# Stick-breaking attention: the sums of key blocks 2 and 3 formed on VectorE for three of five score tiles, two weight units' low parts and q's high part issued later

## The chip, the cores and the metric

The kernel runs on one core of one Trainium2 chip. The metric is the device time of one execution in microseconds (us). The engines named here are TensorE (PE; its weight loads are shown apart as PEld), VectorE (DVE), ScalarE (ACT), GpSimd (POOL) and SyncE (SP, which issues the DMAs).

## What is computed

A decoder of two layers on 512 tokens of width 1024: a Mamba-2 layer, then a layer of stick-breaking attention, each with a gated convolutional feed-forward and an embedding gate. The change lies in the attention alone, 16 heads of 64:

```
for blk in range(seq // SB_BLOCK):                    # 4 blocks of 128 queries
    z = einsum("bthd,bshd->bhts", q[:, q0:q1], k[:, :q1]) * scale
    causal = (q0 + arange(SB_BLOCK))[:, None] > arange(q1)[None, :]
    log_beta = log_sigmoid(z)
    log_keep = where(causal, log_sigmoid(-z), 0.0)
    log_rest = cumsum(log_keep, axis=3, reverse=True) - log_keep
    w = where(causal, exp(log_beta + log_rest), 0.0)
    outs.append(einsum("bhts,bshd->bthd", w, v[:, :q1]))
```

Each weight takes the sum of `log_keep` over all later keys. That sum runs over the rest of the key's own block of 128 and over all of the later blocks.

## The kernel before

*Precision.* Every float32 operand of a matmul is split into a high part, rounded to the type that TensorE reads (`fp32r`), and a low part, the remainder. A product is three matmuls: high by low, low by high, high by high (L241 to L243). Weights come by DMA in units of eight 128x128 blocks (`raw`). For the attention GpSimd multiplies them by a gain (L108), ScalarE makes the high part `whi` (L126), VectorE the low part `wlo` (L133). Three buffers exist for each of `raw`, `whi` and `wlo`, so a unit's DMA starts when the low part of the unit three before it is done.

*The stage.* `pair(p, ...)` runs eight times, once for two heads. Keys lie on the partitions and queries on the columns. There are five score tiles `zs` of 128x512: tile 0 holds key block 2 of both heads (256 columns each), tiles 1 and 2 hold blocks 3 and 1 of one head each (128 and 384 columns), tiles 3 and 4 hold block 0 of one head each (512 columns). A pair goes so:

1. `scores` (L792): score matmuls of all tiles on TensorE, with the mask.
2. ScalarE forms `e`, VectorE adds `max(z, 0)` to it (`sums`, L910). That is the negative of `log_keep`, up to the mask.
3. `parts` (L915) splits `e`: VectorE casts to `sh`, GpSimd subtracts for `sl`.
4. `att_b` (L830): TensorE adds to each score tile the sum over later keys. For the tile's own block that is a matmul of `ntri` (a triangle of -1) with `sh` and `sl`, for each later block one of `nones` (all -1). The table `more` lists these: columns of the score tile from, to, the operand pair and its first column. `s2`, `sa`, `sc` are the parts of tiles 0, 1, 2. Then ScalarE takes the exponential, which gives the weights `w`, and makes their high parts. VectorE makes the low parts afterwards.
5. `att_c` (L863): TensorE multiplies weights and values, for the pair before, within the next pair.

Between these TensorE runs the projections of the next pair: its k product behind the first `att_c`, its q product ahead of `att_b`, its v product behind `att_b`. So in pairs 1 to 6 TensorE's order is scores, `att_c` (head 0), k, `att_c` (head 1), q (with the transposes of the values in it), `att_b`, v. Pair 0 has no `att_c` yet; pair 7 has no projections left and runs parts of the output product instead.

*What sets the order.* Within the eight pairs the order on TensorE, VectorE, ScalarE and GpSimd is that of the program text (a manual schedule for four engines). Each engine takes its queue strictly in that order. What this change moves is therefore visible in `pair`: `parts(3)`, `parts(4)`, then q's evacuation from PSUM (`qk_evac`, L755, into `t`) and its high part on ScalarE, then `att_b`, then a list of low parts on VectorE (`wt.low`, `low`), and at the end the values' evacuation (`v_evac`, L770). `order` gives the sequence of the tiles in `att_b`: 1, 0, 2, 3, 4 in pairs 1 to 6, and 2, 1, 0, 3, 4 in pairs 0 and 7. `new` are the three weight units fetched in a pair: the next pair's values, then k and q of the pair after.

Of the kernel before, what the change touches and what calls it, by code (L numbers as in the profile page):

```python
# [15 lines left out]
P = 128  # L16
# [130 lines left out]
def tile_yoco(ctx: ExitStack, tc: tile.TileContext, xT, pT, prm, cst, csb, wdt, wts, out, dbg=None):  # L147
# [605 lines left out]
    def qk_evac(acc, scale):  # L753
        t = S("t", 2)
        V.scalar_tensor_tensor(out=t, in0=acc, scalar=scale, in1=n_kv.r, op0=ALU.mult, op1=ALU.mult)  # L755
        return t

    def high(src):
        hi = H(F32R, name="hi")
        A.copy(out=hi, in_=src)  # L760
        return src, hi

    def low(src, hi, lo=None):
        lo = lo or H(F32R, name="lo")
        V.tensor_tensor(out=lo, in0=src, in1=hi.bitcast(F32), op=ALU.subtract)  # L765
        return hi, lo

    def v_evac(p, acc):
        vs[p] = S("t", 2, name="v")
        V.tensor_tensor(out=vs[p], in0=acc, in1=n_kv.r, op=ALU.mult)  # L770
# [56 lines left out]
    def like(n, t):  # L827
        return t.rearrange("p (a b) -> p a b", a=2) if n == 0 else t

    def att_b(zs, sp, order):  # L830

        s2, sa, sc = sp[0], sp[1], sp[2]
        more = {
            1: [(384, 512, sa, 0), (256, 512, s2, 0)],
            0: [(128, 256, sa, 0), (384, 512, sc, 0)],
            2: [(384, 512, sc, 0), (256, 512, s2, 256)],
            3: [(128, 512, sa, 128), (256, 512, s2, 0), (384, 512, sa, 0)],
            4: [(128, 512, sc, 128), (256, 512, s2, 256), (384, 512, sc, 0)],
        }
        ws = {}  # L840
        for n in order:
            z = zs[n]
            if n:
                mm = [(z, ntri, s_) for s_ in sp[n]]
                for c0, c1, t_, f0 in more[n]:
                    mm += [(z[:, c0:c1], nones, s_[:, f0:f0 + c1 - c0]) for s_ in t_]
            else:
                mm = [(z[:, i], ntri, s_[:, i * 256:(i + 1) * 256]) for s_ in sp[n] for i in range(2)]
                for c0, c1, t_, f0 in more[n]:
                    i, c = divmod(c0, 256)  # L850
                    mm += [(z[:, i, c:c + c1 - c0], nones, s_[:, f0:f0 + c1 - c0]) for s_ in t_]
            for k, (o_, l_, r_) in enumerate(mm):
                PE.matmul(o_, lhsT=l_, rhs=r_, start=False, stop=k == len(mm) - 1, skip_group_check=True)  # L853
            w = S("d", 6, name="w") if n < 3 else S("c", 3, name="w")
            A.activation(out=like(n, w), in_=z, func=AF.Exp)
            ws[n] = high(w)
        return ws

    o_t = []
# [37 lines left out]
    def pair(p, ws, accs):  # L897
# [7 lines left out]
        def exps(n):  # L905
            es[n] = S("d", 6, name="e") if n < 3 else S("c", 3, name="e")
            A.activation(out=like(n, es[n]), in_=zs[n], func=AF.Abs)  # L907
            A.activation(out=es[n], in_=es[n], func=AF.Exp, scale=-1.0)  # L908
# [6 lines left out]
        def parts(n):  # L915
            sp[n] = H(F32R, name="sh"), H(F32R, name="sl")
            V.tensor_copy(out=sp[n][0], in_=es[n])  # L917
            G.tensor_tensor(out=sp[n][1], in0=es[n], in1=sp[n][0].bitcast(F32), op=ALU.subtract)  # L918

        exps(2)  # L920
        exps(0)
        if p == 7:
# [48 lines left out]
        parts(4)  # L971
        if p < 7:
            wt.high(new[1])
            qt = high(qk_evac(acc, 0.125))
        order = (1, 0, 2, 3, 4) if 0 < p < 7 else (2, 1, 0, 3, 4)
        ws = att_b(zs, sp, order)
        wt.low(new[0])
        ws[order[0]] = low(*ws[order[0]])
        if 0 < p < 7:
            ks[p + 1] = low(*kt)  # L980
        ws[order[1]] = low(*ws[order[1]])
        if p < 7:
            qs[p + 1] = low(*qt)
        ws[order[2]] = low(*ws[order[2]])
        if p:
            o_t.append(low(*oh, lo=S("ot", 8, F32R)))
        ws[3] = low(*ws[3])
        if p < 7:
            wt.low(new[1])
            wt.high(new[2])  # L990
        ws[4] = low(*ws[4])
        if p < 7:
            wt.low(new[2])
            v_evac(p + 1, proj("v", p + 1))
        return ws

    qa, ka = aux_bank("qa"), aux_bank("ka")
# [151 lines left out]
```

## Time and profile before

| | |
|---|---|
| Median of 3 runs | 1525.64 us (1523.31 to 1528.34) |
| The profiled execution | 1525.47 us, its span 1523.6 us |
| TensorE busy | 1490.8 us, 98% of the span |
| VectorE busy | 983.3 us, 65% |
| ScalarE busy | 771.1 us, 51% |
| GpSimd busy | 315.5 us, 21% |
| Mean granted clock of TensorE | 0.995 of full speed |

The eight pairs of the attention lie between 830.8 and 1049 us of the span. The shares are means over stages with different limits, so the attention is read by itself: how full TensorE is there, what it waits for, and at what time the other engines finish what it waits for. Ends of matmuls are modelled; the starts are what the rows are read by.

### The profile page before, as it was taken

The page shows a single profiled execution, that of the slowest core. Times are in us where ns is not written, and L with a number is a line of the kernel's source. Part 1 is how long each engine was busy: PE and PEld are TensorE (multiplying, and loading weights), DVE is VectorE, ACT ScalarE, POOL GpSimd, SP SyncE. Part 2 cuts the span into 40 slices and gives each one's busy share as a digit, 9 for nine tenths or more (in the row PEclk, how much of TensorE's full clock was granted, in tenths as well). Part 3 has the DMA queues.
Part 4 walks back from the last instruction along what each step waited for, and adds up shares of the span by engine and source line. Part 5 has one row for each costly group of instructions (what it writes and reads, how often), then busy time and mean ns, then how long its engine had stood idle before and what let it go on. Part 6 is the DMA issues. An engine that isn't in the chain of part 4 may idle for free.

```text
span 1523.6 us, 18513 instructions
## 1 busy us (share of the span) xinstructions
PE 1490.8 (98%) x7140; PEld 1226.6 (81%) x7140; DVE 983.3 (65%) x1338; ACT 771.1 (51%) x1186; POOL 315.5 (21%) x225
## 2 busy tenths in 40 slices
PE   8999999999999999999999999998999999999997
PEld 5878777788888888888888888887888888888886
DVE  6987888864577777732366676775677677742344
ACT  5466565643344444422356788886444444432243
POOL 0022332532111111100113444521311111100111
PEclk9999999999999999999999999999999999999999
DMA  5334333333333333333332112122233333333321
GB/s 186 95 126 132 103 104 118 104 97 97 91 98 91 104 92 102 102 105 97 97 89 83 42 56 69 42 66 72 89 100 96 98 96 98 97 104 97 97 83 55
DMA packets 43624, 143.69 MB, mean 94 GB/s; under 512 B 4848, under 2 KB 5104, under 8 KB 43536
## 3 DMA queue, kind: packets, MB, share of 16 engines
q1 hardware_dynamic: 43536, 142.51, 30.8%
q8 instruction: 56, 0.92, 0.3%
q14 instruction: 32, 0.26, 0.1%
HBM read 140.32 MB, written 2.16 MB: 94 GB/s over the span
## 4 chain that ended last, share of the span: by engine, by line
PE 73%; ACT 8%; DVE 8%; POOL 5%; issue 5%; DMA 1%; SPq 0%; POOLq 0%; DVEq 0%; ACTq 0%
PE acc L241 22%; PE acc L242 22%; PE acc L243 22%; PE z L853 1%; DVE wlo L133 1%; POOL y L543 1%; DVE c L347 1%; ACT e L908 1%; ACT d L515 1%; DVE e L911 1%; ACT e L907 1%; POOL d L519 1%; ACT whi L126 1%; POOL xrd L479 1%; PE z L821 1%
## 5 line engine op out<-in xcount | busy, mean ns | idle before, releaser
L242 PE MATMUL acc<-lo,whi 128*128 128x512 f32 x1808 | 704.9, 390 | 0.0
L241 PE MATMUL acc<-hi,wlo 128*128 128x512 f32 x1776 | 703.9, 396 | 0.0
L243 PE MATMUL acc<-hi,whi 128*128 128x512 f32 x1776 | 693.3, 390 | 0.0
L133 DVE TENSOR_TENSOR wlo<-raw,whi 128x1024 fp32r<-128x1024 f32 (+1 forms) x241 | 308.5, 1280 | 190.2 <-ACT whi L126 186.5
L242 PEld LDWEIGHTS acc<-lo,whi 128*128 128x128 f32 x1808 | 340.3, 188 | 70.8 <-issue 2.9
L243 PEld LDWEIGHTS acc<-hi,whi 128*128 128x128 f32 x1776 | 334.2, 188 | 70.8
L241 PEld LDWEIGHTS acc<-hi,wlo 128*128 128x128 f32 x1776 | 334.3, 188 | 70.4 <-issue 3.2
L126 ACT CAST whi<-raw 128x1024 fp32r<-128x1024 f32 (+1 forms) x241 | 251.9, 1046 | 270.5 <-PE acc L243 212.4
L347 DVE SCALAR_TENSOR_TENSOR c<-t,pm,c 128x511 f32<-128x511 f32 (+2 forms) x248 | 186.7, 755 | 5.1 <-ACT c L342 1.2
L260 POOL TENSOR_TENSOR acc_sq<-acc_sq,sq 128x512 f32<-128x512 f32 x53 | 76.9, 1451 | 406.1 <-ACT sq L257 357.7
L665 POOL TENSOR_TENSOR hf<-th,c 128x512 f32<-128x512 f32 x44 | 57.4, 1305 | 422.1 <-DVE c L347 411.0
L342 ACT ACTIVATE c<-t,pm 128x512 f32<-128x512 f32 x112 | 91.2, 815 | 26.0 <-DVE t L340 25.7
L222 ACT CAST hi<-hf 128x512 fp32r<-128x512 f32 x44 | 27.1, 620 | 123.2 <-POOL hf L665 123.2
L340 DVE TENSOR_TENSOR t<-acc,r 128x512 f32<-128x512 f32 x112 | 76.5, 684 | 17.8 <-PE acc L243 14.3
L223 DVE TENSOR_TENSOR lo<-hf,hi 128x512 fp32r<-128x512 f32 x44 | 30.4, 690 | 72.1 <-ACT hi L222 72.1
L918 POOL TENSOR_TENSOR sl<-e,sh 128x512 fp32r<-128x512 f32 x40 | 59.6, 1499 | 71.7 <-DVE sh L917 70.6
L662 ACT ACTIVATE th<-c 128x512 f32<-128x512 f32 x44 | 27.8, 632 | 78.3 <-DVE c L347 78.3
L108 POOL TENSOR_TENSOR raw<-raw,pm 128x1024 f32<-128x1024 f32 x20 | 39.2, 1960 | 56.4 <-DMA raw<-in_wts 48.1
L663 DVE SCALAR_TENSOR_TENSOR th<-th,c 128x512 f32<-128x512 f32 x44 | 30.4, 692 | 30.6 <-ACT th L662 30.6
L911 DVE SCALAR_TENSOR_TENSOR e<-z,e 128x512 f32<-128x512 f32 x40 | 26.7, 685 | 32.8 <-ACT e L939 32.6
L515 ACT ACTIVATE d<-d,tok 128x128 f32<-128x128 f32 x128 | 43.5, 390 | 7.2 <-DMA d<-rows 7.1
L765 DVE TENSOR_TENSOR lo<-w,hi 128x512 fp32r<-128x512 f32 x40 | 37.2, 938 | 11.8 <-ACT hi L760 11.8
(205 smaller groups left out, 1481.4 us busy)
## 6 DMA issues: line engine op xcount, KB each, us to landing
raw<-in_wts SPq DMA_DIRECT2D x239, 512.0 KB, 3.6
d<-rows SPq DMA_DIRECT2D x32, 256.0 KB, 4.3
x_k<-in_xT SPq DMA_DIRECT2D x16, 256.0 KB, 5.4
out<-yo SPq DMA_DIRECT2D x3, 512.0 KB, 3.3
p_k<-in_pT SPq DMA_DIRECT2D x4, 256.0 KB, 2.8
raw<-in_wts SPq DMA_DIRECT2D x2, 256.0 KB, 4.4
out<-yo SPq DMA_DIRECT2D x2, 256.0 KB, 4.0
pm<-in_prm SPq DMA_DIRECT2D x1, 312.0 KB, 6.4
```

Source lines behind the costliest of these rows:

```text
L126: self.nc.scalar.copy(out=self.units[u][0][:, part], in_=raw[:, part])
L133: self.nc.vector.tensor_tensor(out=lo[:, part], in0=raw[:, part], in1=hi[:, part].bitcast(F32), op=ALU.subtract)
L241: PE.matmul(acc, lhsT=wl, rhs=xh, start=start and n == 0, stop=False)
L242: PE.matmul(acc, lhsT=wh, rhs=xl, start=False, stop=False)
L243: PE.matmul(acc, lhsT=wh, rhs=xh, start=False, stop=stop and n == len(ks) - 1)
L260: self.eng.tensor_tensor(out=self.acc, in0=self.acc, in1=t, op=ALU.add)
L340: V.tensor_tensor(out=t, in0=acc, in1=r, op=ALU.mult)
L342: A.activation(out=c, in_=t, func=AF.Identity, scale=w[:, f * taps + taps - 1:f * taps + taps], bias=b[:, f:f + 1])
L347: V.scalar_tensor_tensor(out=c[:, s:], in0=t[:, :T - s], scalar=w[:, i:i + 1], in1=c[:, s:], op0=ALU.mult, op1=ALU.add)
L515: A.activation(out=d[:, cs], in_=d[:, cs], func=AF.Relu, scale=-1.0, bias=acs[:, c * 32 + h:c * 32 + h + 1])
L665: G.tensor_tensor(out=hf, in0=th, in1=c1, op=ALU.mult)
L918: G.tensor_tensor(out=sp[n][1], in0=es[n], in1=sp[n][0].bitcast(F32), op=ALU.subtract)
```

## The change

Five things are done in `pair` and `att_b`.

- A new function `cross` runs behind `parts(4)`. For each head VectorE adds block 2's and block 3's `e` on queries 384 to 511 (two adds of 128x128 into `x2`), casts the 128x256 result to a high part and subtracts for the low part. The pair is `sp["x"]`, named `sx`.
- In `more`, tiles 3 and 4, and tile 2 where the order begins with 1, use it: block 2's matmuls cover only queries 256 to 383, and on queries 384 to 511 `sx` stands for blocks 2 and 3 together.
- q's evacuation stands behind `cross`. Its high part is made inside `att_b`, behind the weights of the second tile (`between`).
- The low part of the unit `new[1]` moves from ahead of the last tile's low part to behind the values' evacuation.
- The low part of `new[2]` moves from ahead of the values' evacuation to behind it.

```diff
-    def att_b(zs, sp, order):
-
-        s2, sa, sc = sp[0], sp[1], sp[2]
+    def att_b(zs, sp, order, between):
+
+        s2, sa, sc, sx = sp[0], sp[1], sp[2], sp["x"]
         more = {
             1: [(384, 512, sa, 0), (256, 512, s2, 0)],
             0: [(128, 256, sa, 0), (384, 512, sc, 0)],
-            2: [(384, 512, sc, 0), (256, 512, s2, 256)],
-            3: [(128, 512, sa, 128), (256, 512, s2, 0), (384, 512, sa, 0)],
-            4: [(128, 512, sc, 128), (256, 512, s2, 256), (384, 512, sc, 0)],
+            2: [(256, 384, s2, 256), (384, 512, sx, 128)] if order[0] == 1 else [(384, 512, sc, 0), (256, 512, s2, 256)],
+            3: [(128, 512, sa, 128), (256, 384, s2, 0), (384, 512, sx, 0)],
+            4: [(128, 512, sc, 128), (256, 384, s2, 256), (384, 512, sx, 128)],
         }
...
             ws[n] = high(w)
+            if len(ws) == 2:
+                between()
         return ws
...
+        def cross():
+
+            x, x2 = H(F32R, name="sx"), H(name="x2")[:, 0:256]
+            hi, lo = x[:, 0:256], x[:, 256:512]
+            for i in range(2):
+                V.tensor_tensor(
+                    out=x2[:, i * P:(i + 1) * P], in0=es[0][:, i * 256 + P:(i + 1) * 256], in1=es[1 + i][:, 0:P],
+                    op=ALU.add,
+                )
+            V.tensor_copy(out=hi, in_=x2)
+            V.tensor_tensor(out=lo, in0=x2, in1=hi.bitcast(F32), op=ALU.subtract)
+            sp["x"] = hi, lo
...
         parts(4)
         if p < 7:
             wt.high(new[1])
-            qt = high(qk_evac(acc, 0.125))
+        cross()
+        if p < 7:
+            qt = [qk_evac(acc, 0.125)]
         order = (1, 0, 2, 3, 4) if 0 < p < 7 else (2, 1, 0, 3, 4)
-        ws = att_b(zs, sp, order)
+        ws = att_b(zs, sp, order, lambda: qt.append(high(qt.pop())) if p < 7 else None)
...
         if p < 7:
-            qs[p + 1] = low(*qt)
+            qs[p + 1] = low(*qt[0])
...
         ws[3] = low(*ws[3])
         if p < 7:
-            wt.low(new[1])
             wt.high(new[2])
         ws[4] = low(*ws[4])
         if p < 7:
+            v_evac(p + 1, proj("v", p + 1))
+            wt.low(new[1])
             wt.low(new[2])
-            v_evac(p + 1, proj("v", p + 1))
         return ws
```

Lines behind these are shifted in the changed kernel: `sums` is L913 there, the cast in `parts` L919, the two adds L927, the cast L931 and the subtraction L932 of `cross`.

VectorE, from the values' split to the first weights' low part, in a pair from 1 to 6. Before:

```order
L785 TENSOR_TENSOR vv<-pv,vv 128x4x64 x2
L917 CAST sh<-e 128x512 x2
L755 SCALAR_TENSOR_TENSOR t<-acc,r 128x512
L133 TENSOR_TENSOR wlo<-raw,whi 128x1024
L765 TENSOR_TENSOR lo<-w,hi 128x512
```

The same place now:

```order
L785 TENSOR_TENSOR vv<-pv,vv 128x4x64 x2
L919 CAST sh<-e 128x512 x2
L927 TENSOR_TENSOR x_7773<-e 128x128 x2
L931 CAST sx<-x_7773 128x256
L932 TENSOR_TENSOR sx<-x_7773,sx 128x256
L755 SCALAR_TENSOR_TENSOR t<-acc,r 128x512
L133 TENSOR_TENSOR wlo<-raw,whi 128x1024
L765 TENSOR_TENSOR lo<-w,hi 128x512
```

Four instructions stand between the casts of tiles 3 and 4 and q's evacuation.

TensorE, the tile 2 of `att_b` and the start of tile 3 in pair 2 (z_7265 is tile 2; sh_7384, sh_7402 and sh_7392 are parts of tiles 2, 1 and 0, sh_7446 of tile 3; cr_6544 holds `ntri` and `nones`). Before:

```order
L853 MATMUL z_7265<-sh_7384,cr_6544 128x512
L853 MATMUL z_7265<-sl_7385,cr_6544 128x512
L853 MATMUL z_7265<-sh_7384,cr_6544 128x128
L853 MATMUL z_7265<-sl_7385,cr_6544 128x128
L853 MATMUL z_7265<-sh_7392,cr_6544 128x256
L853 MATMUL z_7265<-sl_7393,cr_6544 128x256
L853 MATMUL z_7266<-sh_7446,cr_6544 128x512
```

The same tile now (z_7277 is tile 2, z_7278 tile 3):

```order
L853 MATMUL z_7277<-sh_7396,cr_6544 128x512
L853 MATMUL z_7277<-sl_7397,cr_6544 128x512
L853 MATMUL z_7277<-sh_7404,cr_6544 128x128
L853 MATMUL z_7277<-sl_7405,cr_6544 128x128
L853 MATMUL z_7277<-sx_7467,cr_6544 128x128 x2
L853 MATMUL z_7278<-sh_7458,cr_6544 128x512
```

The last two matmuls of tile 2 read `sx`, with 128 columns instead of 256.

VectorE, the end of a pair from 1 to 6, from `ot`'s low part to the next pair's first instruction. Before:

```order
L765 TENSOR_TENSOR ot<-e,hi 128x512
L765 TENSOR_TENSOR lo<-w,hi 128x512
L133 TENSOR_TENSOR wlo<-raw,whi 128x1024
L765 TENSOR_TENSOR lo<-w,hi 128x512
L133 TENSOR_TENSOR wlo<-raw,whi 128x1024
L770 TENSOR_TENSOR v<-acc,r 128x512
L891 TENSOR_TENSOR e<-pav,tp 64x512
```

Now:

```order
L765 TENSOR_TENSOR ot<-e,hi 128x512
L765 TENSOR_TENSOR lo<-w,hi 128x512 x2
L770 TENSOR_TENSOR v<-acc,r 128x512
L133 TENSOR_TENSOR wlo<-raw,whi 128x1024 x2
L893 TENSOR_TENSOR e<-pav,tp 64x512
```

Both weight units' low parts stand behind the values' evacuation.

## Rows read from the trace of the kernel before

**Rows 1.** Windows: stretch, length, busy us (instructions) per engine, PEclk, DMA, GB/s; pair 4.
```profile
914.24:942.35 28.11, 28.04 (x164) 23.88 (x162) 19.39 (x29) 23.29 (x37) 13.24 (x8) 1.00 0.20 57
```

**Rows 2.** Waits of TensorE's weight loads, 830 to 1075: us in total, times, longest.
```profile
PEld z L853 <- POOL sl L918: 6.7, 12, 1.2
```

**Rows 3.** Timeline of TensorE, pair 4: start, duration, line, operation, [idle before].
```profile
932.80 0.27 PE L853 MATMUL z<-sh,cr 128*128 128x128 f32 x1
932.91 0.27 PE L853 MATMUL z<-sl,cr 128*128 128x128 f32 x1
...
933.70 0.33 PE L853 MATMUL z<-sh,cr 128*128 128x256 f32 x1
...
933.99 0.40 PE L853 MATMUL z<-sh,cr 128*128 128x512 f32 x1
...
935.21 0.44 PE L853 MATMUL z<-sh,cr 128*128 128x512 f32 x1
935.72 0.50 PE L853 MATMUL z<-sl,cr 128*128 128x512 f32 x1
936.06 0.34 PE L853 MATMUL z<-sh,cr 128*128 128x384 f32 x1
...
936.41 0.29 PE L853 MATMUL z<-sh,cr 128*128 128x256 f32 x1
936.54 0.28 PE L853 MATMUL z<-sl,cr 128*128 128x256 f32 x1
...
936.83 0.45 PE L241 MATMUL acc<-hi,wlo 128*128 128x512 f32 x1
...
946.51 0.44 PE L241 MATMUL acc<-hi,wlo 128*128 128x512 f32 x1
```

**Rows 4.** Timeline of GpSimd, pair 4.
```profile
932.10 1.34 POOL L918 TENSOR_TENSOR sl<-e,sh 128x512 fp32r<-128x512 f32 x1 [0.81 <-DVE sh L917]
933.39 2.28 POOL L918 TENSOR_TENSOR sl<-e,sh 128x512 fp32r<-128x512 f32 x1
938.39 2.00 POOL L108 TENSOR_TENSOR raw<-raw,pm 128x1024 f32<-128x1024 f32 x1 [2.73 <-ACT hi L760]
```

**Rows 5.** Timeline of VectorE, pair 4.
```profile
931.54 0.75 DVE L917 CAST sh<-e 128x512 fp32r<-128x512 f32 x2
932.21 0.68 DVE L755 SCALAR_TENSOR_TENSOR t<-acc,r 128x512 f32<-128x512 f32 x1
932.80 1.71 DVE L133 TENSOR_TENSOR wlo<-raw,whi 128x1024 fp32r<-128x1024 f32 x1
...
938.55 2.38 DVE L765 TENSOR_TENSOR lo<-w,hi 128x512 fp32r<-128x512 f32 x1
...
942.07 1.21 DVE L133 TENSOR_TENSOR wlo<-raw,whi 128x1024 fp32r<-128x1024 f32 x1
```

**Rows 6.** Timeline of VectorE, pair 7.
```profile
1044.58 2.31 DVE L133 TENSOR_TENSOR wlo<-raw,whi 128x1024 fp32r<-128x1024 f32 x1
...
1046.82 2.29 DVE L133 TENSOR_TENSOR wlo<-raw,whi 128x1024 fp32r<-128x1024 f32 x1
```

**Rows 7.** Groups of VectorE by line and shape: count, busy us, mean ns, idle before.
```profile
L192 DVE TENSOR_TENSOR wdr<-wg,wdr 128x256 fp32r<-128x256 f32 x1 | 0.4, 419 | 0.0
...
L407 DVE TENSOR_TENSOR tmp<-tmp 128x128 f32<-128x128 f32 x1 | 0.3, 284 | 0.0
```

**Rows 8.** Timeline of TensorE behind pair 7's scores, in the output product.
```profile
1051.57 0.50 PE L242 MATMUL acc<-ot,whi 128*128 128x512 f32 x1 [1.95 <-DVE ot L765]
...
1052.13 0.55 PE L241 MATMUL acc<-hi,wlo 128*128 128x512 f32 x1
...
1055.78 0.40 PE L241 MATMUL acc_o<-hi,wlo 128*128 128x512 f32 x1
```

**Rows 9.** Windows, columns as in rows 1: behind that pause, and across another.
```profile
1052.00:1054.00 2.00, 2.00 (x7) 1.57 (x6) 0.72 (x2) 0.00 (x0) 0.00 (x0) 0.55 0.12 49
222.00:225.00 3.00, 0.91 (x5) 0.34 (x3) 2.50 (x4) 1.50 (x4) 1.99 (x2) 1.00 0.00 0
```

## The prediction

> **What bounds the kernel now.** The windows view comes first. Cut at the first score matmul of a pair of heads, pair 4 takes 28.11 us with 28.04 us of TensorE work in it at a granted clock of 1.00 [rows 1]; pairs 1 to 6 all look like it. So TensorE's queue sets a pair's period, and an edit in this stage pays only by what it takes out of that queue, or costs what it makes the queue wait. The waits view then shows what TensorE still waits for there: the low parts `sl` that GpSimd makes [rows 2]. In pair 4 that is the second matmul of the last score tile. It starts 0.51 us after the first, 935.21 to 935.72, where 0.23 is usual for 512 columns, and the one behind it takes 0.34 instead of 0.23 to restart [rows 3]. So the chain beside TensorE (exponentials on ScalarE, sums on VectorE, low parts on GpSimd) ends 0.3 us later than TensorE asks: what lengthens that chain is paid at once.
>
> **The place of the new work.** GpSimd makes tile 3's and tile 4's `sl` back to back, from 932.10 to 933.44 and from 933.39 to 935.67 [rows 4]. The first took 1.34 us, the second 2.28. On VectorE there are, in the same time, two `sh` casts to 932.29, q's evacuation at 932.21 (0.68), and the `wlo` of a weight unit that was queued at 932.80 and took 1.71 us, where a free one takes 1.21 (at 942.07) [rows 5]. I read these as turns. The `wlo` has two operands in SBUF; it could not begin before tile 3's `sl` let go, so it began at 934.51 - 1.21 = 933.30. Tile 4's `sl` could not begin before the `wlo` let go (934.43, by the 0.08 us by which successive VectorE instructions overlap), and ended 1.24 us later. Who is next when one lets go? The one that waits on the other engine: at 938.39 GpSimd's multiply cut in ahead of VectorE's next `lo`, which then took 2.38 us [rows 4, 5], and in pair 7 two `wlo` queued one behind the other took 2.31 and 2.29 us [rows 6], with GpSimd's two `sl` between them. The evacuation, with one operand in PSUM, ran through at its usual length.
>
> The Trainium skill, SBUF — State Buffer, section "SBUF: two separate sides", has this as a rule: VectorE and GpSimd share a port pair under an exclusive lock for a whole instruction, and the loser fully blocks; it does not share the bandwidth. By that rule the new work costs what is summed below; if both engines ran on at half speed instead, `sx` would come 2 x 1.2 us after 932.2, at 934.6, and the price would be that of rival 2. The trace agrees with the lock: the 2.28 us are 1.04 of standing still and 1.24 of work.
>
> **The change, part by part.**
>
> *Removed from TensorE.* In tiles 3 and 4, and in tile 2 of pairs 1 to 6, two matmuls of 256 columns become two of 128: 768 columns less in each of six pairs. By the columns alone (512 take 0.23) that would be 0.34 us a pair. The starts say otherwise. A 256-column matmul takes 0.12 to 0.13 us to the next start (936.41 to 936.54), and a 128-column one behind another of 128 takes 0.11 (932.80 to 932.91) [rows 3]. Every matmul here loads its weights anew, and below 256 columns the load sets the pace. So tiles 3 and 4 save 0.01 to 0.02 us each; tile 2, whose two 256-column ones take 0.29 (933.70 to 933.99), saves 0.07. **0.1 us a pair** is all, some 0.7 us in the kernel.
>
> The Trainium skill bears on this too: TensorE: Matmul & The Clock Gate, section "LDWEIGHTS (loading the stationary operand)", puts a load at columns over 1.2 GHz, 107 ns for 128, which is the spacing of the rows; that page's back-to-back gap by moving columns alone would make the saving 0.34 us a pair and the sum below 1.2 us smaller.
>
> *Added on VectorE.* Four instructions a pair, queued between the last `sh` cast and q's evacuation. No row shows these forms; the nearest stand for them [rows 7]. An add of 128x128 takes 0.28 us, a two-input operation of 128x256 takes 0.42. A cast of 128x512 takes 0.42 as well (two in 0.75 [rows 5]), so a cast passes two columns while a two-input operation passes one, and 128x256 cast should take an add's 0.28. Cast and subtraction each wait for the instruction ahead of them, some 0.04 us. Alone that is 1.2 us. But all four read SBUF, and they fall where GpSimd runs both `sl`. On pair 4's clock:
> - The first add is queued at 932.2, begins at 933.30, ends at 933.58 and lets go at 933.50.
> - Tile 4's `sl` waits since 933.39, goes next and ends 1.24 later at 934.74; it lets go 0.09 before its end, as tile 3's did (933.39 against 933.30).
> - The second add runs from 934.65 to 934.93, the cast to 935.25, the subtraction to 935.71.
>
> The order matters little: if both adds come ahead of `sl`, or none does, the same pieces follow one another and the subtraction ends between 935.5 and 935.8.
>
> *The new wait.* In pairs 1 to 6 the tiles come in the order 1, 0, 2, 3, 4, and tile 2 is the first to read `sx`. TensorE asks for it at 933.70, where tile 2's last 256-column pair stands now [rows 3]. It gets the low part at 935.76 (0.05 after its end, as with `sl`): a wait of 2.0 us. Queued behind it are tile 3, tile 4 and the values' projection. Then follow that matmul with the restart (0.06 + 0.11), tile 3 (933.99 to 935.21 is 1.22, less 0.01) and tile 4 (as long, now without its own wait): 935.76 + 0.17 + 1.21 + 1.21 = 938.35. Now the projection begins at 936.83 [rows 3]. So **a pair gets 1.5 us longer**. Bounds: 1.3 with the shorter pieces; 1.8 if the cast takes 0.42 and each gap 0.1.
>
> *Pair 0* has the order 2, 1, 0, 3, 4 and first reads `sx` in tile 3, where TensorE asks late enough to lose only 0.3 us more than it loses now.
>
> *Pair 7* has that order too, and its scores end about as before. But its two `wlo` stand behind the cross sums, and behind them the low part of `ot`, for which TensorE waits until 1051.57 [rows 8]. Turn by turn: first add from 1045.68, `sl` to 1047.12, the rest to 1048.10, the two `wlo` to 1050.36, where they end at 1049.11 now [rows 6]: **1.25 us later**, bare on the path.
>
> *Moved: q's high part.* ScalarE's table load and first two exponentials come ahead of it and no longer wait for q's evacuation; that itself moves to 935.7. The third exponential, behind the cast, comes no later than now. I cost it at nothing: the next scores need q's low part, made by 939.8, only at 943.9. Without that cover it would show as a wait of the score matmuls.
>
> *Moved: two units' low parts.* The `wlo` of the next k and q go behind the values' evacuation; their buffers come free later, so their DMAs start later. The next k product stands 9.68 us behind the start of the values' projection (936.83, 946.51 [rows 3]), at 948.0 on the new clock; its `wlo` is done by 946.0. The first unit's `wlo`, behind the cross sums too, ends at 937.5, and the values' projection reads it at 938.35. Both fit, and nobody waits for the earlier evacuation. So 0, at worst a few tenths a pair.
>
> *Sum*, against the profiled execution, 1525.47 us (span 1523.6 and 1.9 around it; the median of the runs is 1525.64): 6 x 1.52 = 9.1, plus 0.3, plus 1.25: **1525.5 + 10.7 = 1536.2 us**, 0.7% slower.
>
> **Rivals.**
>
> 1. *Nothing blocks, and it gets faster.* If operations this small slip in beside `sl`, the cross sums end at 933.5, before TensorE asks, and no `wlo` stands ahead of tile 4's `sl`, which ends at 934.7. Each of six pairs gains 0.1 + 0.28 + 0.11 = 0.49 us, pair 0 some 1.0, pair 7 loses 0.2: 1525.5 - 3.7 = 1521.8. For it: the evacuation did run beside `sl`. Against: that has an operand in PSUM, and each two-SBUF operation in rows 5 and 6 that met a GpSimd one stood still. It decides if `sx` is there before 933.8.
> 2. *VectorE keeps its turn through all four.* Then the subtraction ends at 934.56, the projection begins at 934.61 + 0.17 + 2.42 = 937.2, and a pair costs 0.37 us: 1525.5 + 2.2 + 1.1 = 1528.8, within what can't be told from no change. Against: cast and subtraction wait for the instruction ahead, a gap in which GpSimd stands ready, and in rows 6 the turn was lost even between two that were ready.
> 3. *The wait slows TensorE's clock as well.* Behind the pause that ended at 1051.57 the clock fell to 0.55 [rows 9], its lower level of 1.2 GHz; nine matmuls took 3.65 us (1052.13 to 1055.78 [rows 8]) instead of 2.04, 1.6 us lost. A pause of like length, at 222, left it at 1.00 [rows 9]. The new waits come six times: 1536.2 + 3.2 = 1539.4 if the clock falls behind two of them, 1545.8 behind all.
>
> **How the numbers follow.** Forecast, with at most one fall of the clock, 0.69; rival 3 with two or more 0.13; rival 2 0.11; rival 1 0.07. About 0.3%, 4.6 us, is what a measurement of this kernel can tell from no change. The forecast's own bounds are 6 x 1.3 + 1.0 = 8.8 and 6 x 1.8 + 2.2 + 1.6 = 14.6, so 1534 to 1540. The range takes in rival 2 and most of rival 3, 1528 to 1544, and leaves out rival 1 and the worst of rival 3. Slower by over 0.3%: forecast and rival 3, less a little for a price half as large, 0.80. Within 0.3%: rival 2, that remainder and most of rival 1, 0.18. Faster by over 0.3%: 0.02, rival 1 with somewhat shorter pieces.
>
> **What would show it.** Right: in pairs 1 to 6 a TensorE wait of about 2 us before `z<-sx`, released by VectorE's L932; one of the two adds at L927 stretched to over 1 us, and tile 4's `sl` among the four; no wait left at tile 4's `sl` matmul; a period of 29.6 us; in pair 7 the wait for `ot` ended near 1.25 us later. Wrong: adds of 0.28 us that run while `sl` runs, or `sx` done by 933.8 on pair 4's clock and the projection no later than now; a new wait at the values' projection for `wlo`, or at the scores for q's low part.

## The result, and the profile after

The changed kernel takes 1547.9 us (median of 4 runs, 1545.7 to 1550.6) against 1525.1 for the kernel before in the same comparison: a ratio of 1.0149, 95% interval 1.0134 to 1.0163. That is 1.5% slower. The direction was forecast, the size was not: 1536.2 with a range to 1544.0. The profiled run took 1545.74 us, its span is 1543.9 us against 1523.6, so 20.3 us are to be found.

The windows of the changed kernel, cut at the first score matmul of each pair (pairs 1 to 6), answer to [rows 1]; length, busy us of each engine, and the granted clock behind them:

```profile
860.16:889.86 29.70, 28.21 (x164) 24.05 (x162) 20.46 (x32) 23.29 (x37) 13.00 (x8) 1.00 0.17 54
889.86:921.11 31.25, 29.76 (x163) 25.45 (x162) 22.16 (x32) 23.39 (x37) 12.39 (x9) 0.95 0.17 51
921.11:952.36 31.25, 29.76 (x163) 25.37 (x162) 20.46 (x32) 23.49 (x37) 12.43 (x8) 0.95 0.16 51
952.36:982.02 29.66, 28.14 (x164) 23.97 (x162) 20.46 (x32) 23.29 (x37) 13.03 (x8) 1.00 0.18 54
982.02:1013.26 31.24, 29.76 (x163) 25.49 (x162) 22.16 (x32) 23.39 (x37) 12.68 (x9) 0.95 0.16 51
1013.26:1044.52 31.26, 29.74 (x163) 25.33 (x162) 20.46 (x32) 23.49 (x37) 6.51 (x5) 0.95 0.17 51
```

There are two lengths, not one. Where the clock stayed at 1.00 a pair takes 29.7 us, 1.56 more than before. Where it reads 0.95 a pair takes 31.25, and the further 1.57 us go with it. TensorE is no longer busy all through: 28.2 of 29.7 us.

What it waits for now, from the waits view of TensorE and of its weight loads, 830 to 1085 (us in total, times, longest), answering to [rows 2]:

```profile
PE z L853 <- DVE sx L931: 9.7, 8, 1.4
PE acc L242 <- DVE ot L765: 1.3, 1, 1.3
PE acc L241 <- DVE wlo L133: 0.2, 1, 0.2
PEld z L853 <- DVE sx L931: 10.8, 8, 1.5
```

The wait for GpSimd's `sl` is gone from pairs 1 to 6, and VectorE's cross sums `sx` stand in its place, in all eight pairs. Their chain on VectorE and what GpSimd does beside it (timelines of the two engines; the last two lines are GpSimd's) answer to [rows 4, 5]. The pair is the same; counted from 0, as in "pairs 1 to 6", it is pair 3, though the rows and the prediction call it pair 4:

```profile
939.09 1.38 DVE L927 TENSOR_TENSOR x<-e 128x128 f32<-128x128 f32 x1
...
940.39 1.36 DVE L927 TENSOR_TENSOR x<-e 128x128 f32<-128x128 f32 x1
...
941.78 0.29 DVE L931 CAST sx<-x 128x256 fp32r<-128x256 f32 x1
942.10 0.43 DVE L932 TENSOR_TENSOR sx<-x,sx 128x256 fp32r<-128x256 f32 x1
942.45 0.68 DVE L755 SCALAR_TENSOR_TENSOR t<-acc,r 128x512 f32<-128x512 f32 x1
943.05 1.22 DVE L133 TENSOR_TENSOR wlo<-raw,whi 128x1024 fp32r<-128x1024 f32 x1
...
936.86 1.29 POOL L920 TENSOR_TENSOR sl<-e,sh 128x512 fp32r<-128x512 f32 x1 [0.46 <-DVE sh L919]
938.98 2.61 POOL L920 TENSOR_TENSOR sl<-e,sh 128x512 fp32r<-128x512 f32 x2 [0.83 <-DVE sh L919]
```

Both 128x128 adds stood still beside one `sl` each, 1.1 us of 1.37, while the two `sl` took 2.61 us together, 1.30 each, which is within 0.02 us of the length of one alone (1.29, at 936.86). The turns are those of the forecast: tile 3's `sl`, first add, tile 4's `sl`, second add. The casts end 6.88 us later here than in the rows (939.17 against 932.29); with that added, the forecast has the first add end at 940.46, tile 4's `sl` at 941.62 and the second add at 941.81, and the rows have 940.47, 941.59 and 941.75. From the end of the casts (939.17) to `sx` (942.53) it is 3.36 us, 3.42 were forecast.

The Trainium skill, SBUF — State Buffer, section "SBUF: two separate sides", says that the engine that loses the shared port blocks fully. These rows agree: 1.38 us for an add that takes 0.28 where GpSimd is quiet (below, 283 ns in two of the experiments).

On TensorE the two lengths part behind the pause. First pair 1, then pair 2 (timeline of TensorE from the last matmul before the pause):

```profile
879.54 0.28 PE L853 MATMUL z<-sl,cr 128*128 128x128 f32 x1
881.18 0.79 PE L853 MATMUL z<-sx,cr 128*128 128x128 f32 x2 [1.36 <-DVE sx L931]
...
883.35 0.39 PE L853 MATMUL z<-sl,cr 128*128 128x512 f32 x1
...
909.23 0.28 PE L853 MATMUL z<-sl,cr 128*128 128x128 f32 x1
910.86 0.79 PE L853 MATMUL z<-sx,cr 128*128 128x128 f32 x2 [1.36 <-DVE sx L931]
...
913.29 0.73 PE L853 MATMUL z<-sh,cr 128*128 128x512 f32 x1
913.82 0.63 PE L853 MATMUL z<-sl,cr 128*128 128x512 f32 x1
```

The pauses are alike to 0.01 us. Behind the first, a 512-column matmul of tile 4 takes 0.39 us (modelled), behind the second 0.63. The windows of the second place, around and behind the pause, show the granted clock (third number from the end):

```profile
911.00:912.00 1.00, 0.87 (x5) 0.64 (x5) 1.00 (x3) 0.54 (x2) 0.00 (x0) 1.00 0.00 0
912.00:916.00 4.00, 4.00 (x17) 3.76 (x16) 4.00 (x7) 2.91 (x6) 0.00 (x0) 0.57 0.44 126
```

It fell to 0.57 on the mean of the second stretch, near its lower level of 1.2 GHz, over 1.1 us after work had begun again (912.0 against 910.86), and stayed low through most of what was left of tiles 3 and 4.

**Where the 20.3 us are.** Pair 0 starts 1.40 us later than before (832.17 against 830.77), before any of the changed work. Pair 0 is 0.75 longer (27.99 against 27.24). Pairs 1 to 6 together are 184.36 us against 168.70, 15.66 more: 6 x 1.56 for the wait and 4 x 1.57 for the clock make 15.64. What is left, 2.5 us, is pair 7 and behind it (timeline of TensorE, and windows behind its wait for `sx`):

```profile
1065.33 0.94 PE L853 MATMUL z<-sx,cr 128*128 128x128 f32 x2 [0.74 <-DVE sx L931]
...
1070.46 0.80 PE L242 MATMUL acc<-ot,whi 128*128 128x512 f32 x1 [1.32 <-DVE ot L765]
```

```profile
1065.70:1070.40 4.70, 3.36 (x10) 2.65 (x10) 4.70 (x8) 2.62 (x5) 0.00 (x0) 0.50 0.48 127
1070.40:1076.00 5.60, 5.54 (x13) 4.39 (x14) 1.21 (x3) 0.44 (x1) 0.00 (x0) 0.51 0.21 83
```

The matmul that waits for `ot` stands 25.94 us behind the pair's start (1044.52) instead of 24.86 [rows 8], 1.08 us. The clock had fallen ahead of it, behind a pause of only 0.74 us, and stays low to 1076. The matmul 14 places behind the one that waits for `ot` starts 5.85 us after it instead of 4.91, so the clock takes 0.9 us more here than it took before [rows 9]. The last 0.4 us lie at the end of the program, where the clock falls in both traces.

### The profile page after: what moved, and what is told of

Its sections match the earlier page's. It is cut to its first block, busy times and chain, and to the rows that moved or that the text cites. A ratio compares the mean times of both kernels' runs of the same rounds, so it can differ in the third digit from the quotient of the medians.

```text
span 1543.9 us, 18537 instructions
## 1 busy us (share of the span) xinstructions
PE 1501.5 (97%) x7140; PEld 1235.9 (80%) x7140; DVE 997.2 (65%) x1370; ACT 771.9 (50%) x1186; POOL 310.0 (20%) x225
## 4 chain that ended last, share of the span: by engine, by line
PE 69%; DVE 11%; ACT 9%; issue 5%; POOL 4%; DMA 1%; SPq 0%; POOLq 0%; DVEq 0%; ACTq 0%
PE acc L241 21%; PE acc L242 21%; PE acc L243 21%; ACT e L910 2%; DVE e L913 2%; PE z L853 2%; ACT e L909 1%; DVE x L927 1%; DVE wlo L133 1%; POOL y L543 1%; DVE c L347 1%; ACT d L515 1%; DVE sh L919 1%; ACT whi L126 1%; POOL xrd L479 1%
## 5 line engine op out<-in xcount | busy, mean ns | idle before, releaser
L241 PE MATMUL acc<-hi,wlo 128*128 128x512 f32 x1776 | 704.4, 397 | 0.2 <-DVE wlo L133 0.2
L133 DVE TENSOR_TENSOR wlo<-raw,whi 128x1024 fp32r<-128x1024 f32 (+1 forms) x241 | 300.7, 1250 | 191.1 <-ACT whi L126 187.4
L241 PEld LDWEIGHTS acc<-hi,wlo 128*128 128x128 f32 x1776 | 334.5, 188 | 70.6 <-issue 3.2
L662 ACT ACTIVATE th<-c 128x512 f32<-128x512 f32 x44 | 27.8, 632 | 78.3 <-DVE c L347 78.3
L920 POOL TENSOR_TENSOR sl<-e,sh 128x512 fp32r<-128x512 f32 x40 | 52.0, 1309 | 71.5 <-DVE sh L919 70.4
L913 DVE SCALAR_TENSOR_TENSOR e<-z,e 128x512 f32<-128x512 f32 x40 | 26.8, 686 | 32.6 <-ACT e L954 32.4
L257 ACT ACTIVATE sq<-x_k 128x512 f32<-128x512 f32 (+1 forms) x50 | 30.6, 616 | 25.9 <-DVE x_k L301 12.9
```

The lines of the kernel that those rows point to most:

```text
L133: self.nc.vector.tensor_tensor(out=lo[:, part], in0=raw[:, part], in1=hi[:, part].bitcast(F32), op=ALU.subtract)
L241: PE.matmul(acc, lhsT=wl, rhs=xh, start=start and n == 0, stop=False)
L913: V.scalar_tensor_tensor(out=like(n, es[n]), in0=zs[n], scalar=0.0, in1=like(n, es[n]), op0=ALU.max, op1=ALU.add)
```

## The experiments

Each line of result gives the median and the ratio to the kernel before from runs on the same chip, with the 95% interval.

### The moves without the sums

```diff
...
-            2: [(256, 384, s2, 256), (384, 512, sx, 128)] if order[0] == 1 else [(384, 512, sc, 0), (256, 512, s2, 256)],
+            2: [(384, 512, sc, 0), (256, 512, s2, 256)],
...
-        cross()
...
```

> The kernel before with the moves alone: q's high part inside the scores' sums and two units' low parts behind the values' evacuation; no sums of blocks 2 and 3. If the blocked sums and the wait behind them are the whole cost: within 1 us of before, TensorE's wait at tile 4's sl as before (0.4 us a pair), period 28.1 us. If the moves carry part of it (later DMAs, a late low part): several us over before, with a wait of TensorE at a projection for wlo.

Measured: 1524.75 us, ratio 0.9992 (0.9981 to 1.0004). Pairs 1 to 6 take 28.09 to 28.12 us. q's high part and the two units' low parts cost nothing where they are put, as forecast; the loss comes with the sums.

### The removed columns alone

```diff
-            2: [(384, 512, sc, 0), (256, 512, s2, 256)],
-            3: [(128, 512, sa, 128), (256, 512, s2, 0), (384, 512, sa, 0)],
-            4: [(128, 512, sc, 128), (256, 512, s2, 256), (384, 512, sc, 0)],
+            2: [(256, 384, s2, 256), (384, 512, sc, 0)] if order[0] == 1 else [(384, 512, sc, 0), (256, 512, s2, 256)],
+            3: [(128, 512, sa, 128), (256, 384, s2, 0), (384, 512, sa, 0)],
+            4: [(128, 512, sc, 128), (256, 384, s2, 256), (384, 512, sc, 0)],
```

> The kernel before with the columns that the change takes off TensorE, and nothing else: in tiles 2, 3 and 4 the passes over 256 columns are made over 128, from what lies there already. What it leaves out: block 2's share in the sums of queries 384 to 511 of these tiles; no work is added on VectorE. Theory (weight loads set the pace of two matmuls under 256 columns, about 0.11 us each either way, as they did in the changed kernel's trace): the pair period stays at 28.11 us within 0.1 us, the wait for tile 4's low part takes up what little is gained, and the time is 1524 to 1526 us, ratio 0.9995 to 1.0005. Rival (columns set the pace): six matmuls in each pair lose 128 columns at 0.053 us, 0.3 us a pair, 2.5 us in all: 1523, ratio 0.9984.

Measured: 1524.7 us, ratio 0.9993 (0.9984 to 1.0002). The same pair as in [rows 1], and what TensorE's weight loads wait for there (windows and waits of this kernel):

```profile
917.26:945.34 28.08, 28.00 (x164) 23.82 (x162) 19.36 (x29) 23.31 (x37) 13.19 (x8) 1.00 0.19 57
PEld z L853 <- POOL sl L918: 7.1, 13, 1.2
```

28.08 instead of 28.11. So 768 columns fewer in a pair are worth 0.03 us. That is little since most of these matmuls follow one another at 0.11 to 0.13 us, with 128 columns or 256 [rows 3], and less than the 0.1 forecast because tile 4's `sl` is no earlier and the wait for it grows (7.1 us against 6.7 in [rows 2]). The change had next to nothing to win at this place.

### The sums formed, but not read

```diff
...
-            3: [(128, 512, sa, 128), (256, 384, s2, 0), (384, 512, sx, 0)],
+            3: [(128, 512, sa, 128), (256, 512, s2, 0), (384, 512, sa, 0)],
...
```

> The changed kernel with the sums still formed on VectorE, but no matmul that reads them (the old table). If the price is TensorE's wait for sx: no wait at the scores' sums longer than before; what is left is q's evacuation and the first wlo pushed back, done some 0.6 us behind TensorE's demand, so +0.6 us a pair, 5 us over before in all (about 1530), and no fall of the clock. If VectorE's added work costs by itself through the chain to the weights and the next pair: nearly as slow as the changed kernel, 1540 or more.

Measured: 1532.7 us, ratio 1.0041 (1.0027 to 1.0054). The adds take 1378 ns on average here too, no matmul waits for them, and yet a pair takes 28.87 us, 0.76 more than before, more than was expected. The wait has moved one place on (waits of TensorE, and pair 3's last score matmul and the first of the values' projection):

```profile
PE acc L241 <- DVE wlo L133: 6.8, 7, 1.5
...
940.02 0.27 PE L853 MATMUL z<-sl,cr 128*128 128x128 f32 x1
941.16 0.47 PE L241 MATMUL acc<-hi,wlo 128*128 128x512 f32 x1 [0.86 <-DVE wlo L133]
```

The weights' low part stands behind the sums and q's evacuation on VectorE, and the values' projection reads it. So half of the 1.56 us would be there whoever reads `sx`: it is the price of 3.4 us more on VectorE. The other half comes from reading it early, in tile 2, with 3.1 us of TensorE's work still behind it (881.18 to 884.32 in the changed kernel's pair 1).

### The sums read late

```diff
-            2: [(256, 384, s2, 256), (384, 512, sx, 128)] if order[0] == 1 else [(384, 512, sc, 0), (256, 512, s2, 256)],
+            2: [(256, 384, s2, 256), (384, 512, sx, 128)] if False else [(384, 512, sc, 0), (256, 512, s2, 256)],
```

> The changed kernel, but tile 2 reads its low part as in the kernel before; only tiles 3 and 4 read the sums of blocks 2 and 3, some 0.6 us later. Theory (the clock falls behind a pause of 1.3 us or more of TensorE; what is left of the pause is shorter): the sums still take 1.37 us each, TensorE waits 0.6 to 0.9 us for them, no pair or one falls below clock 1.00, pairs take 28.9 us, the time is 1530 to 1534 us, ratio 1.003 to 1.006. Rival (the clock falls for another reason, such as the burst of short matmuls behind the pause): clock 0.95 in most pairs, which then take over 30 us, and a time of 1538 us or more.

Measured: 1533.2 us, ratio 1.0049 (1.0035 to 1.0062), pairs of 28.85 to 28.90 us, all six at clock 1.00 (windows of pairs 2 and 3):

```profile
890.82:919.71 28.89, 28.45 (x164) 24.11 (x162) 20.49 (x32) 23.29 (x37) 13.11 (x9) 1.00 0.18 56
919.71:948.60 28.89, 28.42 (x163) 24.10 (x162) 20.49 (x32) 23.29 (x37) 12.20 (x9) 1.00 0.17 55
```

The sums are as slow as in the changed kernel (1378 ns an add) and are still read in every pair; what differs is the pause. In these pairs TensorE is idle for 0.4 to 0.5 us in all, less than the 0.6 to 0.9 expected for `sx` alone, and the clock does not fall. The rival laid the fall to the short matmuls behind the pause. Those of tiles 3 and 4 are the same here, and no pair falls; in the next experiment tile 2's are there as well, and no pair falls either. So it fails.

### The pause filled

Six matmuls with zero weights (`zer`) into the same bank stand ahead of the first that reads `sx` (three in pairs 0 and 7); they add nothing to what is computed.

```diff
+    zer = const.tile([P, P], F32R, name="zer")
+    A.activation(out=zer, in_=ident, func=AF.Identity, scale=0.0)
...
+                    if t_ is sx and n == (2 if order[0] == 1 else 3):
+                        mm += [(z, zer, sa[0])] * (6 if n == 2 else 3)
                     mm += [(z[:, c0:c1], nones, s_[:, f0:f0 + c1 - c0]) for s_ in t_]
```

> The changed kernel with idle TensorE time filled: six matmuls of 512 columns with zero weights ahead of the first that reads sx (three in pairs 0 and 7), which add nothing to the result. If TensorE's pause lets its clock fall and that costs 1.57 us in each of 4 to 6 pairs: every pair at 29.7 us and a granted clock of 1.00, 1537 to 1540. If the clock falls for another reason: no faster than the changed kernel, or slower by the added matmuls.

Measured: 1536.4 us, ratio 1.0062 (1.0042 to 1.0082). `sx` comes as late as in the changed kernel, and every pair takes the shorter of its two lengths (windows of pairs 2 and 3, which fell there):

```profile
888.35:918.07 29.72, 29.59 (x169) 25.01 (x168) 20.49 (x32) 23.28 (x37) 12.87 (x9) 1.00 0.18 54
918.07:947.77 29.70, 29.57 (x170) 25.00 (x168) 20.48 (x32) 23.29 (x37) 13.01 (x9) 1.00 0.17 54
```

It came out a little under its own expectation. It is the forecast's case, a wait and no fall in pairs 1 to 6, and takes the forecast's time, 1536.2. That they agree to 0.2 us is in part luck: the wait (1.59 us a pair) and pair 0 (0.77) were each 0.4 to 0.5 us in all over their terms. With the pause filled, no pair falls though `sx` is as late, so in these pairs it is TensorE's idle time that the fall follows. What the falls are worth is read within the traces, 1.57 us for a pair. The medians of the two comparisons lie 1547.9 - 1536.4 = 11.5 us apart, but that holds pair 0's later start and what lies in and behind pair 7 as well; the second comparison of the changed kernel (below) is only 5.6 us above this one.

### The sums ahead of the casts

```diff
+        cross()
         parts(3)
         parts(4)
...
-        cross()
```

> The sums of blocks 2 and 3 stand ahead of the casts of tiles 3 and 4, where GpSimd has no sl running. If the adds of 1.37 us each are adds that stand still beside sl: 0.28 us each here, sx there before TensorE asks, no wait at sx; the casts come 1.2 us later instead, and with the wlo between the two sl tile 4's sl comes 1.2 us later: period about 29.2 us, 1532 to 1535, clock at 1.00. If the adds are slow by themselves (128 columns out of a strided tile): still 1.37 us each, and slower than the changed kernel.

Measured: 1537.2 us, ratio 1.0066 (1.0044 to 1.0089); later than expected. The adds are quick, since GpSimd is quiet then, but the casts start 1.2 us later and GpSimd's two low parts with them (group of the adds; GpSimd's two in pair 3):

```profile
L927 DVE TENSOR_TENSOR x<-e 128x128 f32<-128x128 f32 x16 | 3.9, 283 | 0.0
...
937.04 3.55 POOL L920 TENSOR_TENSOR sl<-e,sh 128x512 fp32r<-128x512 f32 x2 [2.03 <-PE z L853]
```

And there the `wlo` stands ahead of tile 4's `sl` again: 3.55 us for two, as before. A pair takes 29.26 us, 1.15 more: the chain to tile 4's `sl` was the late one already, so 1.2 us ahead of it are 1.15 us of time. That is the period that was expected, 29.2. What the expectation left out is pair 0, 1.14 us longer, and pair 7 with what lies behind it, 2.4 us longer.

### Tiles 3 and 4 without GpSimd

```diff
+        for n in (3, 4):
+            sp[n] = H(F32R, name="sh"), H(F32R, name="sl")
+            V.tensor_copy(out=sp[n][0], in_=es[n])
+        cross()
+        for n in (3, 4):
+            V.tensor_tensor(out=sp[n][1], in0=es[n], in1=sp[n][0].bitcast(F32), op=ALU.subtract)
-        parts(3)
-        parts(4)
...
-        cross()
```

> The changed kernel with the low parts of tiles 3 and 4 formed on VectorE, behind the sums of blocks 2 and 3, instead of on GpSimd. Theory (the sums are slow because GpSimd's two low parts hold the memory side that both use): the sums take 0.28 us each instead of 1.37, no matmul waits for them, no pair falls below clock 1.00, the wait for tile 4's low part is gone too, and a wait of at most 0.3 us for the weights' low part comes instead; a pair takes 27.8 us, 0.3 less than in the kernel before, and the time is 1522 to 1525 us, ratio 0.998 to 1.000. Rival (the sums are slow by themselves, a short row of 128 columns, or VectorE has simply too much to do): they stay over 1 us, TensorE waits 1 us or more in each pair, the time is above 1532.

Measured: 1523.9 us, ratio 0.9987 (0.9978 to 0.9996). The same sums at the same place (group of the adds, pair 4's window):

```profile
L927 DVE TENSOR_TENSOR x<-e 128x128 f32<-128x128 f32 x16 | 3.9, 283 | 0.0
940.67:968.60 27.93, 27.93 (x163) 23.89 (x162) 20.49 (x34) 23.19 (x37) 11.39 (x7) 1.00 0.18 57
```

0.28 us instead of 1.37, no wait in this pair, and TensorE busy from end to end. The pairs 1 to 6 take 27.92 to 27.95 us, where 27.8 were expected. VectorE does more work here than in the changed kernel and is sooner done: it was not too full, it stood still beside GpSimd.

### The kernel before, tiles 3 and 4 without GpSimd

The same for the kernel before, both low parts behind both casts, without the sums (this edit is shown); and then with the change's moves as well.

```diff
-        parts(3)
-        parts(4)
+        for n in (3, 4):
+            sp[n] = H(F32R, name="sh"), H(F32R, name="sl")
+            V.tensor_copy(out=sp[n][0], in_=es[n])
+        for n in (3, 4):
+            V.tensor_tensor(out=sp[n][1], in0=es[n], in1=sp[n][0].bitcast(F32), op=ALU.subtract)
```

> The kernel before with the low parts of tiles 3 and 4 formed on VectorE, right behind the two casts, instead of on GpSimd, and nothing else. Theory (the end of a pair's middle part is set by what lies between tile 4's cast and its low part: GpSimd's two take 3.6 us, VectorE's two would take 1.2): the wait for tile 4's low part, 0.51 us a pair, is gone, the weights' low part drops from 1.7 to 1.2 us, a pair takes 27.7 us, and the time is 1520 to 1523 us, ratio 0.9965 to 0.9985. Rival (VectorE becomes the bound): TensorE waits for the weights' low part as long as it waited for tile 4 before, a pair stays at 28.1 us, and the time is 1525 to 1527.

> The kernel before with the change's moves alone (two units' low parts behind the values' evacuation, q's high part later) and the low parts of tiles 3 and 4 formed on VectorE; the sums of blocks 2 and 3 are not formed and the old columns stand. It differs from the run with the sums and VectorE's low parts (27.93 us a pair) only in the sums. Theory (in that run the sums take 1.2 us of a VectorE that TensorE does not wait for, and the columns that they save are worth nothing, since weight loads set the pace): a pair takes 27.9 us here too, within 0.1, time 1521 to 1525. Rival (the saved columns are worth their 0.3 us once nothing waits): a pair takes 28.2 us, time 1524 to 1527. Second rival (the sums, 1.2 us, were still on the path there): a pair under 27.7 us, time 1519 to 1522.

Measured: 1522.8 us, ratio 0.9983 (0.9974 to 0.9992), without the moves; 1520.3 us, ratio 0.9971 (0.9959 to 0.9983), with them. Windows of pairs 3 and 4 of the first, then of pair 3 of the second:

```profile
911.10:939.67 28.57, 27.98 (x163) 24.00 (x162) 20.87 (x33) 24.06 (x38) 9.61 (x6) 1.00 0.18 56
939.67:967.50 27.83, 27.83 (x163) 23.89 (x162) 19.32 (x29) 22.53 (x38) 9.64 (x6) 1.00 0.19 57
```

```profile
911.58:939.40 27.82, 27.82 (x163) 23.86 (x162) 18.47 (x30) 23.21 (x37) 9.74 (x6) 1.00 0.18 57
```

Without the moves every second pair takes 28.5 to 28.9 us, where 27.7 were expected in each: VectorE does the two `wlo` ahead of the values' evacuation, and in three pairs the next product, which needs the bank that this frees, waits for it, 2.0 us in all (a wait of `acc` L241 for `v` L770). Why it is every second one is open. With the moves all pairs take 27.82, the shortest of any kernel here, 0.29 under the kernel before, and pair 0 25.89 against 27.24. So the change's moves, worth nothing by themselves, are worth something once the wait for `sl` is gone. And the sums, against this run's 27.82, still cost 0.1 us a pair with nothing in their way: neither rival of the second expectation holds. This is the fastest version by its median and its pairs, and faster than both kernels.

### The changed kernel again

> The changed kernel again, for a second trace. Theory (a pair takes 29.7 us, or 31.25 us where the clock falls behind the pause; which pairs fall is chance): periods of those two lengths alone, with the falls at other pairs than the second, third, fifth and sixth; as many falls as the span has over 1535 us divided by 1.57. Rival (the falls are tied to the place in the program): the same four pairs fall.

Measured: 1542.0 us (2 runs), ratio 1.0109 (1.0091 to 1.0128). Pairs 1 to 6 in this trace (windows):

```profile
857.09:888.34 31.25, 29.73 (x164) 25.52 (x162) 22.16 (x32) 23.39 (x37) 12.71 (x9) 0.95 0.17 51
...
919.59:949.27 29.68, 28.18 (x163) 24.00 (x162) 20.46 (x32) 23.32 (x37) 11.71 (x8) 1.00 0.17 54
949.27:980.54 31.27, 29.76 (x164) 25.43 (x162) 22.16 (x32) 23.41 (x37) 12.94 (x9) 0.95 0.16 51
...
1011.80:1041.51 29.71, 28.20 (x164) 23.96 (x163) 20.46 (x32) 23.31 (x37) 6.52 (x5) 1.00 0.18 54
```

The lengths are the same two to 0.02 us, and pairs 1, 2, 4 and 5 fell, where 2, 3, 5 and 6 did in the first trace. So the fall is not tied to a place in the program. It is not quite chance either: in both traces two fall and one does not, in turn. What sets that is open, and the count expected from the span, three, was one short. The two comparisons of this kernel also differ by more than their intervals, 1.0149 against 1.0109. The two traces' spans differ by 4.5 us: pair 0 starts 3.1 us earlier here (829.06), and pair 7 and behind is 1.5 us shorter; the six pairs are alike.

This trace also answers [rows 9]. The pause of 2.09 us at 222, behind which the clock stayed at 1.00 in the trace of before, stands in all twelve traces, 2.07 to 2.10 us long. Here the clock fell behind it (timeline of TensorE, and a window behind it):

```profile
222.67 1.13 PE L486 MATMUL pst<-xrd,btok 128*128 128x512 f32 x2 [2.09 <-POOL xrd L479]
```

```profile
224.00:228.00 4.00, 4.00 (x11) 2.45 (x9) 4.00 (x5) 3.97 (x10) 4.00 (x3) 0.57 0.02 4
```

It fell there with the moves alone and with the sums ahead of the casts too, 0.67 and 0.59 in the same window, and not in the other nine.

## Why the prediction was wrong, point by point

**The bound now** was right. TensorE's queue set the period and tile 4's `sl` ended last in it; the experiment that lengthened the chain to it paid (1.15 us for 1.2), and the ones that took that wait away gained.

**The removed columns** were forecast at 0.1 us a pair; 0.03 were measured alone. Right for its purpose; by the columns alone it would have been 0.34.

**The added work** was forecast at 3.42 us from the casts to `sx` and took 3.36. The lock was the right mechanism: 1.37 us an add beside GpSimd, 0.28 without. The order of the turns was right as well, and each step of it came within 0.06 us of the forecast. Tile 4's `sl` was held up by some 0.02 us (1.30 each for the two, 1.29 alone), where 0.11 were forecast.

**The wait.** 1.52 us a pair were forecast, 1.56 measured in the pairs at clock 1.00, and 1.59 with the pause filled.

**Pair 0** was forecast at 0.3 and took 0.75 us. Its scores read `sx` late, and by that wait alone it would have been some 0.34 us: an estimate, with the values' projection at 854.22, right behind the last score matmuls (from 854.00, 0.22 for two), where it is at 854.62. But the weights' low part stands behind the sums there too, and the values' projection waited 0.23 us for it and restarted behind it. It is the same price as that of pair 0 in the two kernels whose pairs do not read `sx` early, 0.76 and 0.77. A term left out, 0.45 us, once.

**Pair 7** was forecast at 1.25 us and took 1.08 up to the matmul that waits for `ot`; then 0.9 us more by the clock.

**The moves** cost nothing, as forecast.

**Readings of the rows.** What the prediction calls pair 4 is pair 3, counted from 0. And in [rows 6] one of GpSimd's two `sl` lies ahead of the first `wlo`, the other between the two. Neither changes its sum.

**The step that failed is the chance of rival 3.** Its mechanism and price were in the prediction: 1.6 us for a fall, 1.57 measured. But the sum put the clock at nothing, the bounds allowed one fall, and two or more had a chance of 0.13, where four of six pairs fell in both traces, and pair 7 lost by the clock in the first as well. That reasoning set one pause behind which the clock fell beside another, at 222, behind which it did not [rows 9], and from one against one it took the side of the lower price. The second row was no evidence of a kind of pause that leaves the clock alone: the 0.91 of 3 us in it is the pause of 2.09 itself, with matmuls on both sides, and behind that very pause the clock fell in three of twelve traces. One trace shows one outcome of a thing that comes out both ways, and it should not have been read as a rule. What decides between the two no run here shows.

With the four falls alone, 1536.2 + 6.3 = 1542.5, inside the range. The rest of the profiled run is 1.4 us that lie before the changed work, 0.9 of clock behind pair 7, 0.4 at the end of the program and 0.5 of small terms. The 1.4 before it differ from trace to trace: pair 0 starts between 828.5 and 833.9 us in the traces here, and 3.1 us apart in the two of the changed kernel. So how far the forecast missed is in part chance: the second comparison's 1542.0 lies inside its range. The slower two of the four runs, 1549.9 and 1550.6, have no trace; a mean clock of 0.984 against the profiled run's 0.988 suggests more falls in them, which is argued and not shown.

**The rivals.** Rival 1 (nothing blocks) is refuted by the first add of 1.38 us, and rival 2 (VectorE keeps its turn) by the second, 1.36, ahead of which GpSimd had its turn. Rival 3 held, with four falls between its two and six; the time of the first comparison lies above even its price for six, 1545.8, by the terms just named and the two runs without a trace.

## What to carry to other kernels

Before work is put on VectorE, look at what GpSimd does in that stretch: an operation of 0.28 us with both operands in SBUF took 1.37 beside it, and taking GpSimd's part over to VectorE made both kernels faster. A TensorE stage that the queue bounds should not get a pause at all: one of 1.4 us cost 1.57 more through the clock in four pairs of six. So read a new wait's price as wait plus fall, and if the wait can't go, move its reader back or fill it. Do not take one pause that left the clock alone as proof that the next one will. And shortening matmuls of 256 columns that each load new weights to 128 was worth next to nothing, 0.03 us for six.

## What was not expected of the hardware

One pause can go both ways. The same one of 2.07 to 2.10 us, in a part of the program that no edit touches, left the clock at 1.00 in nine traces, and in three the clock fell behind it.

The clock fell behind equal pauses of some 1.36 us in two pairs of every three, in two traces, at different pairs. With some 0.45 us of idle time in a pair it did not fall once in six, behind pauses of 0.87 us (the sums formed, but not read) not once in six, and with the pause filled by matmuls not once either. That is no limit, though: in pair 7 of the first trace it fell behind a pause of 0.74 us. In these pairs 1 to 6 it fell 0.7 to 1.2 us after work had begun again, not in the pause.

Turns between VectorE and GpSimd come out alike for long and for short operations. Between two `sl` of GpSimd a `wlo` of 128x1024 took its turn and held the second `sl` up by 1.04 us [rows 4, 5]; an add of 128x128 took its turn at the same place, and the two `sl` took 2.61 us, 1.30 each against 1.29 alone.
